# A stream of its own for the key projection's weights, woven into the merge of a transformer layer

## The chip, the cores and the metric

The kernel runs on one core of a Trainium2 chip. The metric is the device time of one execution in microseconds (us). Before the change three runs gave 2997.36 to 3000.63 us, with a median of 2999.9 us. For this kernel two times that differ by less than about 0.2% (6 us) can't be told apart.

The engines are named as in the profile: PE multiplies matrices, PEld loads its weights, DVE and ACT work on vectors, POOL is the general engine, SP issues most loads. Each engine takes its instructions strictly in the order of its queue, and an instruction that waits holds up everything behind it.

## The reference

The layer takes 1024 tokens and 256 context tokens, both of width 1024:

```python
h = rmsnorm(x, n1) * (1 + sc1) + sh1
q, k, v, gb, gcv, u, ga, gv = split_proj(h @ w_in)
y_attn = windowed_attention(rope(q), rope(k), v, kc, vc, sink) @ w_attn_out
y_conv = conv_branch(gb, gcv, u, conv_w, w_conv_out)
x = x + g1 * ((sigmoid(ga) * y_attn + sigmoid(gv) * y_conv) @ w_mix_out)
h2 = rmsnorm(x, n2) * (1 + sc2) + sh2
x = x + g2 * peer(h2, pw_q, p_keys, p_u, p_v)
return rmsnorm(x, final_g)
```

`peer` projects each token to 8 heads x 2 halves of 128 query values (`t @ w_q`, 1024 x 2048), scores each half against 128 keys (`sub_keys`), takes the best 16 of each half, the best 16 of their sums, and mixes 16 of 16384 experts per head by a softmax of the scores.

## The kernel before

**Precision by parts.** A float32 operand that PE multiplies is split into two float16 parts, high and low, and a product is three matmuls (`mm3`: high x high, high x low, low x high). For a weight this is done in `weight()`: SP loads a tile `w32` of 128 x 1024 float32 (512 KB), ACT casts it with a scale into the high part (below: the cast), DVE subtracts for the low part (the split), and both parts lie in a tile `whl`. With a key, POOL then issues a store of `whl` into a scratch tensor in HBM; the next call with that key loads the parts from there, by SP, without cast and split. There are two buffers for `w32` and four for `whl`, shared by all weights:

```python
w = self.pw.tile([128, 2, 8, 128], F16, name="whl", tag="whl", bufs=4)
w32 = self.pw.tile([128, 8, 128], F32, name="w32", tag="w32", bufs=2)
```

So a load into `w32` can't be issued before the split of the tile two loads earlier has read its buffer, and a cast can't start before a `whl` buffer is free: after its last matmul and its store.

**Stages.** The 1024 tokens are handled as two halves of 512. Stage 0 makes the modulation and the normed input. Stage 1 makes q, k, v and the convolution branch, woven with the attention of the first 4 of 8 blocks and with the late part of the modulation (the first weave). Stage 2 of half 0 has four pieces: the merge (8 steps of three weights each, `ga`, `gv`, `ac`), which is woven with the attention of blocks 4 to 7 (the second weave); the mixing projection (8 weights `mx`); the norm and modulation to `h2` (8 slices); and the key projection, 16 chunks `c`, each with one weight `wq`. A chunk is 24 matmuls of 128x512 on PE, a split of the product (`qqh` on ACT, `qql` on DVE), 12 short matmuls against a key table `sk` (one for chunks 0 to 7, one for 8 to 15), an eviction `sl` on ACT, and on DVE the search of the best 16 (`MAX`, `MAX_INDEX`, `MATCH_REPLACE`, 20 pieces). Stage 2 of half 1 follows with the same four pieces, beside it the selection and gate building of half 0 on DVE, PE and ACT (`run_side`, `gates`). It finds all weights in scratch. Then come the dense experts, two thirds of the time.

**Order.** `weave` advances several generators in turn, each by its share: with lengths 24 and 36 the merge gets 24 turns to the attention's 36. Within that order the framework's scheduler sets the final order of each engine's queue when the kernel is built. In `attends` the attention runs as a pipeline over 32 heads: scores of one head, transposes of the head before, sum of the head before that; between a head's scores and its transposes lie a maximum on DVE (`mx`, `nm`), an exponential on ACT (`pe`) and a split (`pn` on ACT and DVE).

**In the profile** most records carry line 72, the helper that forwards every call; so they are read by tiles: `whl<-w` on ACT is a cast, `whl<-w,whl` on DVE a split, `w<-w_q` on SP the load of a weight of the key projection.

Of the kernel before, what the change touches and what calls it, by code (L numbers as in the profile page):

```python
# [114 lines left out]
def drain(gen):  # L115
    while True:
        try:
            next(gen)
        except StopIteration as e:
            return e.value  # L120


class K:
# [678 lines left out]
    def natural(self, k):  # L802
# [8 lines left out]
        nc.scalar.activation(hn.rearrange("p a b -> p (a b)"), pt, AF.Copy)  # L811
        nc.sync.dma_start(self.h2d[:, :, k * 128:(k + 1) * 128].rearrange("t p d -> p t d"), hn)

    def scores(self, hf, c, qh, ql, skw):

        nc, p = self.nc, self.ps2
        ps = self.bank()
        for t in range(4):
            ts = slice(t * 128, (t + 1) * 128)
            self.mm3(ps[:, ts], qh[:, ts], ql[:, ts], skw[0][:, c % 8, :], skw[1][:, c % 8, :], True, True)  # L820
        sl = self.px1.tile([128, 4, 128], F32, name="sl", tag="sl", bufs=2)
        nc.scalar.activation(sl.rearrange("p a b -> p (a b)"), ps, AF.Copy, scale=2.0 ** -10)
        h, pp = c // 2, c % 2
        vs = [self.sv[hf][:, t, pp, h, :] for t in range(4)]
        ix = [self.si[hf][:, t, pp, h, :] for t in range(4)]
        for t in range(4):
            nc.vector.max(vs[t][:, 0:8], sl[:, t, :])
        for t in range(4):
            nc.vector.max_index(ix[t][:, 0:8], vs[t][:, 0:8], sl[:, t, :])
        for t in range(4):  # L830
            nc.vector.match_replace(sl[:, t, :], vs[t][:, 0:8], sl[:, t, :], NEG)
        for t in range(4):
            nc.vector.max(vs[t][:, 8:16], sl[:, t, :])
        for t in range(4):
            nc.vector.max_index(ix[t][:, 8:16], vs[t][:, 8:16], sl[:, t, :])
# [572 lines left out]
    def run(self):  # L1408
        nc, a = self.nc, self.a
        self.setup()  # L1410
        self.nsq = 4
        self.g_two, self.two = self.pool("psA", space=PSUM)
        self.g_pa, self.pa = self.pool("ps0", space=PSUM)
        self.nbank = 6
        g_pw, self.pw = self.pool("wts", side="left")
        halves = [None, None]
        self.hT, self.cT, self.aT = [None, None], [None, None], [None, None]
        for hf in (1, 0):
            g, p = self.pool(f"half{hf}", side="left")
            halves[hf] = g  # L1420
            self.hT[hf] = tuple(p.tile([128, 8, HALF], F16, name=f"hT{hf}{i}") for i in range(2))
            self.cT[hf] = tuple(p.tile([128, 4, HALF], F16, name=f"cT{hf}{i}") for i in range(2))
            self.aT[hf] = tuple(p.tile([128, 4, HALF], F16, name=f"aT{hf}{i}") for i in range(2))
        self.stage0()
        g_q, self.pq = self.pool("qkv", side="left")
        self.stage1()
        g_s2, self.ps2 = self.pool("s2", side="right")
        self.sv[0] = self.ps2.tile([128, 4, 2, 8, 16], F32, name="sv0")
        self.si[0] = self.ps2.tile([128, 4, 2, 8, 16], U32, name="si0")
        self.nrstd = 1  # L1430
        self.nsq = 2
        st = self.stage2(0)
        self.weave([(self.until(st, "merged"), 24), (self.attends(4, 8), 36)])
        self.close(g_q)
        self.close(self.g_pa)
        self.close(self.g_two)
        self.g_pa, self.pa = self.pool("psQ", space=PSUM)
        self.nbank = 8
        drain(self.until(st, "summed"))
        st1 = self.stage2(1)  # L1440
        for _ in range(8):
            next(st)
        for _ in range(AHEAD):
            next(st1)
        drain(st)
        self.close(self.g_pa)
        g_pf, self.pf = self.pool("psF", space=PSUM)
        self.ftag = ("f", 2)
        self.nbank = 6
        g_pa, self.pa = self.pool("psB", space=PSUM)  # L1450
        self.close(halves[0])
        g_g = self.open_gate("gate0", "left", 2)
        self.run_side(st1, self.gates(0), GATES_B)
        self.u_first = {i: self.weight(None, a["u_t"][i]) for i in range(UPRE, UPRE + 3)}
        self.close(g_g)
        self.close(self.g_x1)
        self.close(g_s2)
        self.close(halves[1])
        self.close(g_pw)
        self.close(g_pa)  # L1460
        self.close(g_pf)
        g_pv, pv = self.pool("psV", space=PSUM, reuse_waits="tile")
        self.pf, self.ftag = pv, ("v", 3)
        self.bank = self.fbank
        g_pt, self.ppt = self.pool("parts", side="left", reuse_waits="tile")
        g_ac, self.pac = self.pool("acc", side="left", reuse_waits="tile")
        self.part = self.pac.tile([128, 8 - NRES, HALF], F32, name="part")
        gd, pd = self.pool("dense0", side="left", reuse_waits="tile")
        g_g = self.open_gate("gate1", "right", 1)
        self.experts(pd, pv)  # L1470
        self.close(gd)
        self.close(g_ac)
        self.close(g_pt)
        self.close(g_g)
        self.close(g_pv)
        self.close(self.g_pc)
# [63 lines left out]
```

## Time and profile before

| what | value |
|---|---|
| median of 3 runs | 2999.9 us |
| the profiled execution's own time | 2997.38 us |
| its span, first to last instruction | 2995.6 us |
| busy: PE, DVE, ACT, POOL | 95%, 88%, 39%, 35% |
| second weave with its end | 339 to 517 us |
| mixing projection of half 0 | 517 to 561 us |
| norm and modulation of half 0 | 561 to 580 us |
| key projection of half 0 | from 567, searches done at 680.6 us |
| stage 2 of half 1 with the gates | to about 1060 us |

The times in the rows below count from the span's start. The share of busy time over the whole span says little, since the stages have different limits; it is read by stage. A bracket at the end of a row gives the idle time just before the instruction and what ended it.

### The profile page before, as it was taken

Reading aid. Unit: us, or ns where it says so; the run is one execution under the profiler, and the core shown is the slowest. Engines: PE = TensorE matmul, PEld = TensorE weight load, DVE = VectorE, ACT = ScalarE, POOL = GpSimd, SP = SyncE. Lnnn points to the kernel's source line nnn. Section 1 sums busy time; section 2 is a strip of 40 time slices with the busy share of each in tenths; the row PEclk is TensorE's granted clock in tenths of the full one; section 3 lists DMA queues with packets and bytes.
Section 4 is the critical chain, followed back from the end, with each engine's and each line's share of the span. In section 5 each row is a group of like instructions: output and inputs, shape, how many; then the busy total and the mean of one; then the engine's idle time right before and its main releaser. Section 6 shows DMA issues by size and latency. Waiting matters only on the chain.

```text
span 2995.6 us, 49091 instructions
## 1 busy us (share of the span) xinstructions
PE 2858.1 (95%) x18685; PEld 1521.8 (51%) x18685; DVE 2647.2 (88%) x5438; ACT 1176.0 (39%) x1878; POOL 1052.4 (35%) x814
## 2 busy tenths in 40 slices
PE   6899999989989998999999999999999999999998
PEld 2455555444444543444444444444444446776675
DVE  7788776699999999999899999999889979888887
ACT  4844576333434332332333333333333333433432
POOL 3200012201111004444444444544544444455553
PEclk9999999999999998999999999999999999999999
DMA  6233445654445728998999998999989999999995
GB/s 227 92 120 114 127 127 183 215 181 151 176 179 185 255 82 288 315 329 309 331 314 349 352 327 306 338 332 332 351 314 347 324 316 339 360 377 351 354 365 192
DMA packets 327197, 795.74 MB, mean 266 GB/s; under 512 B 22960, under 2 KB 147248, under 8 KB 319792
## 3 DMA queue, kind: packets, MB, share of 16 engines
q1 hardware_dynamic: 219536, 372.08, 37.4%
q0 software_dynamic: 103968, 395.36, 35.7%
q10 hardware_dynamic: 3456, 25.17, 2.1%
q8 instruction: 146, 2.39, 0.3%
q14 instruction: 91, 0.75, 0.1%
HBM read 696.31 MB, written 96.21 MB: 265 GB/s over the span
## 4 chain that ended last, share of the span: by engine, by line
PE 44%; DVE 10%; DMA 4%; issue 3%; POOL 2%; ACT 0%; SPq 0%; DVEq 0%; POOLq 0%; ACTq 0%
PE res L72 23%; PE ups L72 13%; PE vps L72 5%; DVE row L72 4%; DMA row<-u,ci 2%; POOL row L916 2%; PE fbank L72 1%; DVE vl L72 1%; DMA v<-v 1%; DVE ul L72 1%; DVE eq L72 1%; DVE wdl L72 1%; DVE gel L72 0%; DVE part L72 0%; ACT ge L72 0%
## 5 line engine op out<-in xcount | busy, mean ns | idle before, releaser
L916 POOL DMA_INDIRECT row<-u,ci x512 | 669.9, 1308 | 881.1 <-DVE row L72 649.4
L72 DVE SCALAR_TENSOR_TENSOR row<-row,hn 128x1024 f32<-128x1024 f32 x512 | 614.1, 1222 | 62.7 <-DMA row<-u,ci 46.0
L72 PEld LDWEIGHTS <-vh 128*128 128x128 f16 x5120 | 468.4, 98 | 341.4 <-issue 12.5
L72 PE MATMUL res<-wdl,vh 128*128 128x128 f16 (+2 forms) x2176 | 626.2, 305 | 14.3 <-DVE wdl L72 14.1
L72 PE MATMUL res<-wdh,vl 128*128 128x128 f16 (+2 forms) x2176 | 623.1, 305 | 6.7 <-DVE vl L72 6.7
L72 PE MATMUL res<-wdh,vh 128*128 128x128 f16 (+2 forms) x2176 | 622.8, 305 | 0.0
L72 PE MATMUL ups<-h,uh 128*128 128x512 f16 x1952 | 582.4, 380 | 0.0
L72 PEld LDWEIGHTS <-whl 128*128 128x128 f16 x3288 | 317.0, 99 | 368.7 <-issue 47.2
L72 PE MATMUL bank<-hT,whl 128*128 128x512 f16 x1584 | 376.2, 386 | 16.0 <-ACT hT L72 5.7
L72 ACT ACTIVATE vh<-v 128x1024 f16<-128x1024 f32 x248 | 260.3, 1050 | 296.1 <-PE res L72 143.1
L72 PE MATMUL ups<-h,ul 128*128 128x512 f16 x976 | 371.0, 380 | 5.1 <-DVE ul L72 5.1
L72 PEld LDWEIGHTS <-vl 128*128 128x128 f16 x2560 | 250.5, 98 | 197.2 <-DVE vl L72 27.7
L72 PEld LDWEIGHTS <-uh 128*128 128x128 f16 x1952 | 190.9, 98 | 228.5 <-issue 2.7
L72 DVE SCALAR_TENSOR_TENSOR vl<-v,vh 128x1024 f16<-128x1024 f32 x248 | 301.7, 1217 | 0.1
L916 POOL DMA_INDIRECT row<-v,ci x128 | 210.9, 1648 | 179.6 <-DVE wdl L72 90.0
L72 ACT ACTIVATE gel<-ups 128x512 f32<-128x512 f32 x125 | 74.6, 597 | 370.8 <-PE ups L72 341.7
L72 ACT ACTIVATE ge<-fbank 128x512 f32<-128x512 f32 x224 | 122.2, 594 | 245.7 <-PE fbank L72 228.4
L72 ACT ACTIVATE wdh<-gel 128x512 f16<-128x512 f32 x128 | 80.5, 629 | 342.5 <-DVE gel L72 328.1
L72 DVE SCALAR_TENSOR_TENSOR racc<-row,fig,racc 128x1024 f32<-128x1024 f32 x127 | 162.5, 1280 | 10.7 <-DMA row<-v,ci 9.7
L72 DVE TENSOR_TENSOR e<-iotas,ii 128x1024 f16<-128x1024 f16 x224 | 153.0, 705 | 6.9 <-ACT ii L72 4.8
L72 PEld LDWEIGHTS <-ul 128*128 128x128 f16 x976 | 95.7, 98 | 121.9 <-DVE ul L72 6.5
L72 PE MATMUL vps<-wdh,vh 128*128 128x512 f16 x384 | 145.5, 379 | 4.3 <-ACT ge L72 3.6
(223 smaller groups left out, 4191.1 us busy)
## 6 DMA issues: line engine op xcount, KB each, us to landing
v<-v SPq DMA_DIRECT2D x248, 512.0 KB
u<-u_t SPq DMA_DIRECT2D x122, 512.0 KB
gd<-ge POOLq DMA_DIRECT2D x32, 1024.0 KB
gt<-gd SPq DMA_DIRECT2D x32, 1024.0 KB
wm<-w_mod SPq DMA_DIRECT2D x48, 512.0 KB
gd<-ge ACTq DMA_DIRECT2D x24, 1024.0 KB
gt<-gd SPq DMA_DIRECT2D x32, 768.0 KB
w<-w_in SPq DMA_DIRECT2D x34, 512.0 KB
```

The costliest lines, as they stand in the source:

```text
L72: r = f(*args, **kw)
L916: self.nc.gpsimd.indirect_dma_start(out=r, out_offset=None, in_=tab, in_offset=bass.IndirectOffsetOnAxis(ap=ci[:, s:s + 1], axis=0))
```

## The change

A generator `key_weights` calls `weight()` for the two key tables and the 16 weights of the key projection, one per turn, and is woven into the second weave as a third stream with 18 turns. Its result is not kept: what stays is the copy in scratch. When the key projection of half 0 calls `weight()` with the same keys, it finds them there.

```diff
+    def key_weights(self):
+
+        for c in range(18):
+            if c < 2:
+                self.weight(("sk", c), self.a["skT"][c], scale=64.0)
+            else:
+                self.weight(("wq", c - 2), self.a["w_q"][c - 2])
+            yield
@@
-        self.weave([(self.until(st, "merged"), 24), (self.attends(4, 8), 36)])
+        self.weave([(self.until(st, "merged"), 24), (self.attends(4, 8), 36), (self.key_weights(), 18)])
```

So 18 loads, casts, splits and stores move from the key projection (and the end of the mixing projection, where the first were loaded) into the second weave and the end of the first. In the key projection 18 loads of parts from scratch take their place.

The ACT queue in the middle of the second weave, before. `w_5044` and `w_5127` are weights of the merge, `pe` and `pn` belong to the attention, `sgv` and `sa` are gates.

```order
L72 ACTIVATE whl<-w_4920 128x1024
L72 ACT_TABLE_LOAD
L72 ACTIVATE sgv<-bank 128x512
L72 ACTIVATE ao<-sc 128x64
L72 ACT_TABLE_LOAD
L72 ACTIVATE pe,se<-sc,nm 128x640
L72 ACTIVATE whl<-w_5044 128x1024
L72 ACTIVATE pn<-pe 128x640
L72 ACTIVATE whl<-w_5127 128x1024
L72 ACTIVATE mh<-sa 128x512
```

The same place now. `w_4904`, `w_4990` and `w_5121` are weights of the merge, `w_4983` and `w_5114` weights of the key projection.

```order
L72 ACTIVATE whl<-w_4904 128x1024
L72 ACTIVATE whl<-w_4983 128x1024
L72 ACT_TABLE_LOAD
L72 ACTIVATE sgv<-bank 128x512
L72 ACTIVATE ao<-sc 128x64
L72 ACT_TABLE_LOAD
L72 ACTIVATE pe,se<-sc,nm 128x640
L72 ACTIVATE whl<-w_4990 128x1024
L72 ACTIVATE pn<-pe 128x640
L72 ACTIVATE whl<-w_5114 128x1024
L72 ACTIVATE ao<-sc 128x64
L72 ACTIVATE whl<-w_5121 128x1024
```

Five casts stand where three stood, and the attention's `pe` and `pn` stand between and behind them.

The DVE queue in one chunk of the key projection of half 0, before: a split of a weight follows each `qql`.

```order
L72 SCALAR_TENSOR_TENSOR qql<-bank,qqh 128x512
L72 SCALAR_TENSOR_TENSOR whl<-w_6702,whl 128x1024
L72 MAX sv_3545<-sl 128x8 x4
L72 MAX_INDEX si_3546<-sv_3545,sl 128x8 x4
L72 MATCH_REPLACE sl<-sv_3545,sl 128x128 x4
L72 MAX sv_3545<-sl 128x8 x4
L72 MAX_INDEX si_3546<-sv_3545,sl 128x8 x4
```

The same chunk now.

```order
L72 SCALAR_TENSOR_TENSOR qql<-bank,qqh 128x512
L72 MAX sv_3545<-sl 128x8 x4
L72 MAX_INDEX si_3546<-sv_3545,sl 128x8 x4
L72 MATCH_REPLACE sl<-sv_3545,sl 128x128 x4
L72 MAX sv_3545<-sl 128x8 x4
L72 MAX_INDEX si_3546<-sv_3545,sl 128x8 x4
```

The split is gone from every chunk; the rest stands as it stood. PE's queue has the same instructions in nearly the same order.

## Rows read from the trace of the kernel before

**Rows 1.** Busy time by stage: busy us (instructions) per engine, clock, DMA share, GB/s

```profile
180.00:339.00 159.00, 155.80 (x1438) 93.20 (x1437) 137.13 (x240) 67.83 (x136) 2.38 (x4) 1.00 0.40 120
339.00:517.00 178.00, 171.93 (x1571) 99.39 (x1569) 125.65 (x196) 127.02 (x209) 30.13 (x37) 1.00 0.46 142
...
580.00:681.00 101.00, 93.11 (x553) 46.89 (x553) 100.19 (x543) 30.67 (x46) 7.46 (x14) 0.97 0.60 194
681.00:1060.00 379.00, 345.61 (x2425) 182.08 (x2424) 361.99 (x1145) 152.37 (x249) 57.95 (x54) 0.98 0.53 187
```

**Rows 2.** Groups in 580 to 681: busy us, mean ns, then idle before and releaser

```profile
L72 DVE SCALAR_TENSOR_TENSOR whl<-w,whl 128x1024 f16<-128x1024 f32 x14 | 17.1, 1219 | 0.8 <-ACT whl L72 0.8
...
L72 ACT ACTIVATE whl<-w 128x1024 f16<-128x1024 f32 x14 | 14.8, 1054 | 23.9 <-DMA w<-w_q 23.9
...
L72 PE MATMUL bank<-whl,qql 128*128 128x128 f16 x64 | 12.1, 226 | 7.1 <-DVE qql L72 7.1
```

**Rows 3.** Timeline of PE, one chunk of the key projection: start, duration, instruction

```profile
642.23 5.34 PE L72 MATMUL bank<-h,whl 128*128 128x512 f16 x24
...
647.41 0.27 PE L72 MATMUL bank<-whl,qqh 128*128 128x128 f16 x2
...
648.06 0.23 PE L72 MATMUL bank<-whl,qql 128*128 128x128 f16 x1 [0.38 <-DVE qql L72]
...
648.63 5.34 PE L72 MATMUL bank<-h,whl 128*128 128x512 f16 x24
```

**Rows 4.** Timeline at the first and the last chunks of the key projection

```profile
575.45 1.22 DVE L72 SCALAR_TENSOR_TENSOR whl<-w,whl 128x1024 f16<-128x1024 f32 x1
...
577.38 2.33 PE L72 MATMUL bank<-h,whl 128*128 128x512 f16 x10 [0.25 <-DVE h L72]
...
661.43 5.34 PE L72 MATMUL bank<-h,whl 128*128 128x512 f16 x24
...
671.39 0.29 PE L72 MATMUL bank<-whl,qql 128*128 128x128 f16 x1 [3.65 <-DVE qql L72]
...
673.38 7.18 PE L72 MATMUL bank<-hT,whl 128*128 128x512 f16 x24 [0.73 <-ACT sl L72]
...
680.61 0.27 DVE L72 CAST fi<-si 128x256 f16<-128x256 uint32 x1
```

**Rows 5.** Timeline of SP and ACT: two loads of a weight and the casts they release

```profile
622.42 0.33 SPq L172 DMA_DIRECT2D w<-w_q  x1
...
627.69 1.06 ACT L72 ACTIVATE whl<-w 128x1024 f16<-128x1024 f32 x1 [4.78 <-DMA w<-w_q]
...
641.06 0.33 SPq L172 DMA_DIRECT2D w<-w_q  x1
...
645.14 1.06 ACT L72 ACTIVATE whl<-w 128x1024 f16<-128x1024 f32 x1 [3.34 <-DMA w<-w_q]
```

**Rows 6.** Groups of DVE and ACT in the second weave, 339 to 517

```profile
L72 DVE SCALAR_TENSOR_TENSOR whl<-w,whl 128x1024 f16<-128x1024 f32 x23 | 31.3, 1360 | 5.2 <-ACT whl L72 5.1
...
L72 ACT ACTIVATE whl<-w 128x1024 f16<-128x1024 f32 x24 | 25.2, 1051 | 14.7 <-PE bank L72 14.7
L72 ACT ACTIVATE pe<-sc,nm 128x640 f32<-128x640 f32 x23 | 18.2, 794 | 5.0 <-DVE nm L72 4.8
L72 ACT ACTIVATE pn<-pe 128x640 f16<-128x640 f32 x23 | 16.2, 728 | 0.2
L72 ACT ACTIVATE ao<-sc 128x64 f32<-128x64 f32 x32 | 6.9, 217 | 5.3 <-PE sc L72 5.0
```

**Rows 7.** Timeline in the second weave: a cast that waits, and PE behind it

```profile
423.78 1.06 ACT L72 ACTIVATE whl<-w 128x1024 f16<-128x1024 f32 x1 [1.75 <-PE bank L72]
...
425.18 1.72 DVE L72 SCALAR_TENSOR_TENSOR whl<-w,whl 128x1024 f16<-128x1024 f32 x1
...
426.65 0.30 PE L72 MATMUL sc<-kd,q 128*128 128x320 f16 x1 [1.24 <-ACT ao L72]
...
429.25 0.61 PE L72 MATMUL sc<-v,pt 128*128 128x64 f16 x15 [1.78 <-DVE pt L72]
```

## The prediction

> **What bounds the kernel now.** I read the busy times by stage first, then the groups of the two stages that the change touches, then the timelines there. In the second weave PE is busy 171.9 of 178 us, and ACT and DVE 127 and 126: PE sets the pace, with 6.1 us of idle time [rows 1]. In the key projection of half 0 it is the other way round: DVE is busy 100.2 of 101 us, PE 93.1 [rows 1]. The 14 splits in that stretch are 17.1 us of this, and ACT waits 23.9 us for the loads of weights, which costs nothing there, since DVE is late anyway [rows 2]. Half 1 behind it has DVE busy 362 of 379 us and PE 346 [rows 1]: DVE is nearer to full, so what DVE gets back at 680.6 us, where it turns from the searches to the selection [rows 4], should mostly reach the end. The dense stage needs the result of all this and simply starts earlier or later.
>
> **What the change takes out of the key projection.** One chunk takes 648.63 - 642.23 = 6.40 us [rows 3]. PE's own work in it is 5.18 us of projection (642.23 to 647.41) and 12 short matmuls: ten of them take 648.63 - 648.06 = 0.57 us, so 12 about 0.68 [rows 3]; together 5.86. DVE's is 6.40 with the split and 6.40 - 1.22 = about 5.2 without [rows 2, 3]. So PE takes over as the bound at 5.86, and not all of the 18 x 1.22 = 22 us that DVE sheds comes back.
>
> The sum for the stage: the first two chunks run while the modulation still makes `h2`, and their last matmuls end at 577.38 + 2.33 = 579.7 [rows 4]. A split of 1.22 us stands among the modulations at 575.45 [rows 4] and goes: 578.5. Fourteen chunks follow: 14 x 5.86 = 82.0, so PE ends the last projection at 660.5, where it now ends at 661.43 + 5.18 = 666.6 [rows 4]. In the old order PE then waits 3.65 us for `qql` behind the searches and takes 7.18 us for the next 24 matmuls [rows 4], where 5.18 is usual: a stretch at 1.2 instead of 2.4 GHz. With DVE in step the last `qql` follows at once; the two searches left on DVE, of 4.6 us each (the 5.2 without a `qql` of 0.6), end at about 660.5 + 1.2 + 9.2 = 671. That is 10 us before 680.6; PE turns to half 1 some 11 us earlier. I take a gain of 10 us. Bounds: 4, if only the 6.3 us on PE come through and half 1 swallows a third; 22, if all of DVE's relief did. The 18 loads from scratch that stand in place of the old ones are cost at nothing: in half 1 the same loads feed the same chunks, and PE's waits in this kernel's key projections are for DVE and not for a load. If one came late, it would cost up to a load time, 4 to 5 us.
>
> **What it puts into the second weave.** Each moved weight brings a load, a cast, a split and a store; 17 more casts fall between 339 and 517 us (24 now, 41 then; by the queue, the other moves end in the first weave). Busy time: ACT 127 + 17 x 1.05 = 145 us, DVE 126 + 17 x 1.36 = 149 [rows 1, 6], both under 178. Traffic: 142 GB/s x 178 us is 25 MB, and 18 weights of 1.05 MB (load and store) make it 44 MB, or 248 GB/s; by the key projection's 194 GB/s at a share of 0.60 that is a share of about 0.77 [rows 1]. None of this alone is over the limit.
>
> What is near a limit is the loop through the two `w32` buffers. A load was issued at 622.42 and its cast, which waited for it, began at 627.69: 5.3 us; another took 645.14 - 641.06 = 4.1 [rows 5]. Behind the landing come the cast (1.05) and the split: from the cast at 423.78 to the split's end at 426.90 there are 3.1 us [rows 7]; at least it is 1.05 + 1.2 = 2.3. So one buffer comes round in 6.4 to 8.4 us, and a weight passes every 3.2 to 4.2 us, where the weave asks for one every 178 / 41 = 4.3. On the average it holds, but the queue isn't even. Take the piece of the new ACT queue that the change section shows: between the start of the cast of `w_4990` and that of `w_5121` ACT has two casts, a `pn` and an `ao`, 1.05 + 0.73 + 1.05 + 0.22 = 3.05 us [rows 6]; but the load of `w_5121` goes out only behind the split of `w_4990`, 6.4 to 8.4 us before its own cast can start. ACT stands for 3 to 5 us, and behind it wait `mh`, `pe` and `pn`: the softmax of the next heads, on which PE's transposes wait. I went down the queue this way, with 4.5 us for a load and 3.0 for cast and split: 16 of the 41 casts come too soon, by 40 us in all. With 4.1 and 2.4 it is 13 casts and 26 us, with 5.3 and 3.7 it is 19 and 60 us. In the old queue the same count gives 5 us.
>
> How much of it PE feels: casts already wait 14.7 us for buffers [rows 6], and PE idles 6.1 us in all. The rows show the way: a cast waits 1.75 us, and 1.8 us after it ends PE idles 1.24 us for `ao`, then 1.78 us for `pt` [rows 7]. 6.1 / 14.7 = 0.41 us of PE for 1 us of a waiting cast. 40 x 0.41 = 16 us; since ACT's slack shrinks from 51 to 33 us, I take 17. Bounds: 0, if the cover of PE's long projections holds, and 40, if all of it passes through.
>
> The sum: 2997.4 (the profiled execution; its span of 2995.6 and 1.8 around it) - 10 + 17 = 3004.4. The median of the runs is 2.5 above that execution, so 3007 is what I compare with 2999.9.
>
> [...]
>
> **The rivals.**
>
> (1) The weave hides everything: 2997.4 - 10 = 2987, 2990 as a median. For it: in the first weave DVE is busy 137 of 159 us, 86%, and PE still 155.8 (98%) [rows 1], beside steady loads on the same SP queue. Against it: ACT has 68 of 159 us there, and in the new second weave 145 of 178; few of those loads go through cast and split. It decides if PE loses under 4 us in the weave.
>
> (2) A draw: loads near 4.1 us and a prompt DVE, 26 x 0.41 = 11 us lost, 10 gained: 2998, 3001 as a median. For it: the 4.1 us load; against it: the larger share of DMA in the weave.
>
> (3) Heavily slower: ACT falls so far behind that every stall reaches PE, and `whl` buffers, of which four now serve two streams, come late for the merge itself; 40 us lost, 10 gained: 3027, 3030 as a median. It begins where ACT's waits pass its slack of 33 us. For it: PE's clock fell behind a wait of 3.65 us [rows 4], so stalls of that length would cost twice. Against it: PE has 5.18 us of projection between most steps of the attention as cover.
>
> That the change does not do what it says is excluded by the order: no cast and no split is left in the key projection.
>
> **How the numbers follow.** I give the forecast 42%, rival (1) 25%, the draw 22%, (3) 11%. What counts as no change is within 0.2%, 2994 to 3006. The forecast's own range is 3002 to 3015, as its weave loss goes from 12 to 25; about 8 of its 42 points lie under 3006. So slower is 34 + 11 = 45%, the same 22 + 8 = 30%, faster 25%. The range for 8 in 10 reaches down to rival (1), 2989, and up to (3), 3030.
>
> **What would show it.** In the profile after: chunks of the key projection 5.9 us apart and PE busy without a break there, with DVE idle in between; the `CAST` of the selection some 10 us closer to the first chunk. In the second weave: casts that wait for `w<-w_q` and `w<-w_in`, which they don't at all now, in sum some 30 to 40 us; PE idle 20 us and more, before transposes and sums, released by ACT and DVE; the stage from 339 to 534 instead of 517. I am wrong if casts hardly wait for loads, or wait and PE's idle time stays near 6 us: then (1) holds. I am wrong about the gain if chunks stay at 6.4 us, or if half 1 takes up what they save.

## The result and the profile after

The changed kernel takes 3018.55 us (median of 4 runs, 3017.22 to 3019.65), the kernel before, beside it on the same chip, 2998.63 us (4 runs, 2995.23 to 3000.63). The ratio is 1.0067 with a 95% interval of 1.0055 to 1.0079: slower by 20 us, where 7 were predicted (3007, with a range of the forecast itself from 3002 to 3015 and one for 8 in 10 from 2989 to 3030). The profiled execution of the changed kernel took 3017.84 us, with a span of 3016.1.

Where the 20.5 us of the two spans lie (the stages are bounded by first instructions: `sa` of the merge, `mh` into the mixing projection, `qqh` of the key projection, the selection's `CAST`, the first `wdl<-gel` of the dense stage and its last one):

| stage of half 0 | before | after | difference |
|---|---|---|---|
| up to the merge (first weave) | 339.2 | 343.2 | +4.0 |
| second weave | 178.3 | 199.6 | +21.3 |
| mixing projection, norm | 61.2 | 60.1 | -1.1 |
| key projection | 101.9 | 96.1 | -5.8 |
| half 1 with the gates | 409.3 | 406.6 | -2.7 |
| dense stage | 1359.7 | 1365.3 | +5.6 |
| what follows | 546.0 | 545.2 | -0.8 |

The busy times by stage, after; as in [rows 1] the columns are PE, PEld, DVE, ACT and POOL busy, granted clock, DMA share, GB/s:

```profile
343.20:542.80 199.60, 176.56 (x1568) 101.14 (x1567) 142.37 (x209) 137.71 (x220) 38.37 (x54) 0.97 0.65 209
605.00:699.00 94.00, 91.23 (x558) 46.69 (x556) 86.56 (x528) 18.74 (x32) 0.00 (x0) 1.00 0.35 125
```

In the second weave PE is idle for 199.6 - 176.6 = 23.0 us; before it was 178.3 - 171.8 = 6.5, counted the same way. That is 16.5 us of the 21.3. The other 4.8 are in the busy time: the same matmuls take 176.6 instead of 171.8 us, and the granted clock beside them is 0.97 instead of 1.00: it falls to 0.50 (1.2 of 2.4 GHz) in three places, around 400, 445 and 482 us, each beside a wait of PE (2.5, 3.9 and 3.9 us). In the key projection the roles have changed as against [rows 1]: PE is busy 91.2 of 94 us, DVE has idle time.

One chunk of the key projection on PE, after, for [rows 3]:

```profile
641.95 5.34 PE L72 MATMUL bank<-h,whl 128*128 128x512 f16 x24
...
647.80 5.34 PE L72 MATMUL bank<-h,whl 128*128 128x512 f16 x24
```

The chunk takes 647.80 - 641.95 = 5.85 us, without a wait; before it took 6.40. The weights now come from scratch, and two groups in 605 to 699 show what PE waits for:

```profile
L72 PE MATMUL bank<-h,whl 128*128 128x512 f16 x336 | 74.8, 379 | 1.6 <-DMA whl<-ws_wq 1.6
...
L72 PE MATMUL bank<-whl,qql 128*128 128x128 f16 x62 | 11.2, 219 | 0.4 <-DVE qql L72 0.4
```

The 7.1 us of waiting for `qql` [rows 2] are 0.4, and PE waits 1.6 us in all for the loads of parts.

Casts and splits in the second weave, after, for [rows 6]:

```profile
L72 DVE SCALAR_TENSOR_TENSOR whl<-w,whl 128x1024 f16<-128x1024 f32 x39 | 50.5, 1300 | 22.2 <-ACT whl L72 21.9
L72 ACT ACTIVATE whl<-w 128x1024 f16<-128x1024 f32 x40 | 41.5, 1053 | 34.3 <-DMA ws_wq<-whl 22.2 <-PE bank L72 4.5 <-DMA w<-w_ac 4.1
```

And all waits of the casts in 343.2 to 542.8 (us in total, times, longest), with the longest ones of PE:

```profile
ACT whl L72 <- DMA ws_wq<-whl: 22.2, 10, 4.1
PE sc L72 <- ACT ao L72: 6.9, 4, 3.9
PE sc L72 <- ACT pn L72: 5.2, 5, 2.8
PE sc L72 <- DVE pt L72: 4.7, 2, 3.9
ACT whl L72 <- PE bank L72: 4.5, 2, 3.9
ACT whl L72 <- DMA w<-w_ac: 4.1, 2, 2.4
ACT whl L72 <- DMA w<-w_mx: 1.5, 1, 1.5
ACT whl L72 <- DMA w<-w_in: 1.3, 1, 1.3
ACT whl L72 <- DMA w<-w_q: 0.6, 1, 0.6
```

The casts wait for a DMA, but hardly for a load: 7.5 us in four rows. What they wait for is `ws_wq<-whl`, the stores of the new stream, 22.2 us; about half of it, 11 us in five waits, stands in front of casts of the merge, the rest in front of the stream's own (loads and casts paired in their order). For PE, which held their buffers before, they wait 4.5 us instead of the 14.7 of [rows 6]; in all 34.3 instead of 14.7. A store holds its parts buffer `whl` until it has landed, and the next cast wants that buffer. The DMA issues in 343 to 543 (count, KB each, median us from issue to landing) give the time:

```profile
ws_wq<-whl POOLq DMA_DIRECT2D x16, 512.0 KB, 5.4
```

The timeline at the end of the weave shows such a wait and who stands behind it:

```profile
528.16 0.56 POOL L176 DMA_DIRECT2D ws_wq<-whl  x1 [2.54 <-DVE whl L72]
...
533.43 1.06 ACT L72 ACTIVATE whl<-w 128x1024 f16<-128x1024 f32 x1 [4.13 <-DMA ws_wq<-whl]
534.40 0.61 ACT L72 ACTIVATE oh<-ao 128x512 f16<-128x512 f32 x1
...
535.07 0.40 PE L72 MATMUL bank<-id,oh 128*128 128x128 f16 x4 [1.70 <-ACT oh L72]
...
536.41 0.40 PE L72 MATMUL bank<-id,ol 128*128 128x128 f16 x4 [0.94 <-DVE ol L72]
```

The store goes out at 528.16 and the cast begins at 533.43. Behind the cast in ACT's queue stands `oh` of the attention, and PE idles 1.70 us for it, then 0.94 for `ol`, which DVE makes from it.

### The profile page after: what moved, and what is told of

Its sections match the earlier page's. It is cut to its first block, busy times and chain, and to the rows that moved or that the text cites. A ratio compares the mean times of both kernels' runs of the same rounds, so it can differ in the third digit from the quotient of the medians.

```text
span 3016.1 us, 49116 instructions
## 1 busy us (share of the span) xinstructions
PE 2862.5 (95%) x18685; PEld 1524.1 (51%) x18685; DVE 2650.1 (88%) x5438; ACT 1171.0 (39%) x1876; POOL 1057.6 (35%) x814
## 4 chain that ended last, share of the span: by engine, by line
PE 41%; DVE 9%; issue 5%; DMA 4%; POOL 3%; ACT 0%; POOLq 0%; DVEq 0%; ACTq 0%
PE res L72 23%; PE ups L72 12%; PE vps L72 5%; DMA row<-u,ci 3%; DVE row L72 3%; POOL row L925 3%; PE fbank L72 1%; DVE vl L72 1%; DVE ul L72 1%; DVE wdl L72 1%; DVE eq L72 1%; DVE gel L72 0%; ACT ge L72 0%; DVE part L72 0%; DVE acc L72 0%
## 5 line engine op out<-in xcount | busy, mean ns | idle before, releaser
L72 PEld LDWEIGHTS <-vh 128*128 128x128 f16 x5120 | 469.0, 98 | 342.6 <-issue 15.0
L72 ACT ACTIVATE gel<-ups 128x512 f32<-128x512 f32 x125 | 74.6, 597 | 351.0 <-PE ups L72 339.9
## 6 DMA issues: line engine op xcount, KB each, us to landing
gt<-gd SPq DMA_DIRECT2D x32, 1024.0 KB, 12.2
gt<-gd SPq DMA_DIRECT2D x32, 768.0 KB, 10.3
```

What stands on the lines that cost most here:

```text
L72: r = f(*args, **kw)
```

## The experiments

Each was run beside the kernel before; the ratio is to that, with its 95% interval. Theories in the expectations: A, the stores hold the shared parts buffers; B, the loop through the two `w32` buffers (my prediction); C, the plain work of the added casts and splits; D and E are told where they come in. The framework orders the queues anew for each kernel: costonly has the ACT queue of the changed kernel from 300 us to the end of the second weave, operation by operation (250), but in nostore, noload, workonly and ownwhl1 19 to 34 of these stand elsewhere, and on DVE 30 to 51 of some 260 (compared in the traces). What these four give for a part of the stream holds the effect of the other order too, and no run takes the two apart.

**costonly: the stream without its use.** The stores go under other names, so the key projection loads and splits everything as before.

```
-                self.weight(("sk", c), self.a["skT"][c], scale=64.0)
+                self.weight(("zk", c), self.a["skT"][c], scale=64.0)
-                self.weight(("wq", c - 2), self.a["w_q"][c - 2])
+                self.weight(("zq", c - 2), self.a["w_q"][c - 2])
```

> The woven stream does all its 18 loads, casts, splits and stores, but stores under other names, so that the key projection of half 0 loads, casts and splits as in the kernel before. This is the cost alone. If cost and gain are separate and add up, the second weave is as long as in the changed kernel (mixing projection starting near 542 us, PE idle there some 22 us), chunks of the key projection are 6.4 us apart, and the total lies 20 + 10 = 30 us over before. Rival: what the weave loses is partly given back later in any case, and the total is only 20 us over before.

Measured: 3030.41 us, ratio 1.0098 (1.0074 to 1.0122). The second weave, with the columns as above:

```profile
343.80:548.00 204.20, 180.99 (x1565) 103.17 (x1563) 142.15 (x208) 137.79 (x219) 38.63 (x53) 0.94 0.66 210
```

The two parts of the change add up: +31 us for the cost alone, +20 for both, so a gain of about 11 (9.6 by the stages of the two profiles before and after). PE's idle time is that of the changed kernel (23.2 against 23.0 us), while its busy time is 4.4 us longer at a clock of 0.94: with the same order of ACT's queue, the idle time came out alike in the two profiles and the clock did not.

**nostore: the stream without its stores** (their key is `None`); the key projection as before.

```
-                self.weight(("wq", c - 2), self.a["w_q"][c - 2])
+                self.weight(None, self.a["w_q"][c - 2])
```

> The woven stream loads, casts and splits the 18 weights but does not store the parts, and the key projection makes its own again as before. Theory A (a shared buffer of parts is held by the store of a key weight, and a cast of the next weight stands until that store has landed): without stores the casts hardly wait for a buffer, the second weave gets back 15 of the 21 us it lost, the total is some 10 us over before. Theory B (the loop through the two float32 buffers, as I predicted): the weave stays some 20 us longer and the total is near that of the cost alone, 30 over before, with casts waiting for loads. Theory C (just more work on ACT and DVE): as B, but no waits for loads.

Measured: 3011.75 us, ratio 1.0038 (1.0022 to 1.0054). The second weave, and the waits of casts in it:

```profile
340.30:527.80 187.50, 174.81 (x1571) 100.29 (x1570) 140.82 (x211) 140.53 (x224) 31.27 (x38) 0.99 0.55 174
```

```profile
ACT whl L72 <- DMA w<-w_mx: 8.1, 4, 3.8
...
ACT whl L72 <- DMA w<-w_in: 1.8, 2, 0.9
ACT whl L72 <- DMA w<-w_q: 1.7, 2, 0.9
```

Against costonly the weave gets 16.7 us back and the first weave 3.5. With all loads in place and no store it loses only 9.2 us, where theory B expected some 20. The casts wait 12.2 us for loads, with the 0.6 for `w_ac` that is not shown; PE idles 12.7 us, 6.2 more than before.

**noload: the stream without its loads.** One float32 tile of its own is loaded once; 18 casts, splits and stores under other names follow from it. The key projection is as before.

```
+        w32 = self.pk.tile([128, 8, 128], F32, name="w32k", tag="w32k", bufs=1)
+        self.nc.sync.dma_start(w32, self.a["skT"][0])
...
+            self.split(w32, 64.0, w[:, 0], w[:, 1])
```

> The woven stream loads one float32 tile once into a buffer of its own and casts, splits and stores it 18 times, under other names; the key projection makes its own parts as before. So the 17 other loads, and their use of the two shared float32 buffers, are left out. Theory A (stores hold the buffers of parts): the weave is as long as with the loads, total 25 to 30 us over before. Theory B (loads): the weave is back to within 5 us of before, total some 5 us over before. Theory C (work on ACT and DVE): 25 to 30 over before, without waits of casts for stores.

Measured: 3015.05 us, ratio 1.0048 (1.0026 to 1.0069).

```profile
339.30:536.00 196.70, 179.14 (x1548) 102.40 (x1548) 150.13 (x214) 145.69 (x228) 41.60 (x58) 0.95 0.57 188
```

```profile
ACT whl L72 <- DMA ws_z<-whl: 11.2, 6, 2.8
```

The loads are gone and the weave still loses 18.4 us. Two things make this number too large: the profiled execution, 3021.0 us, is the slowest of the five (from 3007.78), and 4.3 us of it are a wait of PE that the edit itself brings (workonly, next). What is left for the loads is told with the table below.

**workonly: neither loads nor stores.** The edit is noload without its store. Theory D had come from the runs so far (ACT's idle time in front of a DMA is what reaches PE, at about a half), and it expected next to nothing here.

> The stream with its 18 casts and splits alone: they read one resident float32 tile, nothing is loaded per weight and nothing is stored; the parts buffers are the shared four, the key projection is as before. Theory D (PE idles some 0.5 us for each us that a cast on ACT stands for a DMA; the bare work costs nothing): casts wait for DMA under 5 us, PE idles 6 to 9 us in the second weave, which takes 178 to 182 us; total 0 to +5 against before (3001 to 3006). Theory C (the work of the added casts and splits on ACT and DVE costs by itself): weave 186 to 190 us as without the stores, total +9 to +12 (3011).

Measured: 3010.96 us, ratio 1.0033 (1.0020 to 1.0046).

```profile
340.40:530.00 189.60, 177.13 (x1548) 101.05 (x1548) 144.69 (x214) 144.61 (x228) 33.17 (x40) 0.96 0.49 148
```

```profile
ACT whl L72 <- PE bank L72: 10.7, 6, 4.5
...
PE bank L72 <- ACT whl L72: 4.3, 1, 4.3
```

The weave loses 11.3 us, as theory C expected, and 6.0 of it are idle time of PE. But the wait of 4.3 us is not plain work. It belongs to this edit and to noload alone, and stands at the head of the stream:

```profile
337.99 1.06 ACT L72 ACTIVATE whl<-w32k 128x1024 f16<-128x1024 f32 x1 [4.51 <-DMA w32k<-skT]
...
343.05 1.04 ACT L72 ACTIVATE whl<-w 128x1024 f16<-128x1024 f32 x1
...
344.15 1.03 PE L72 MATMUL bank<-hT,whl 128*128 128x512 f16 x2 [4.29 <-ACT whl L72]
```

The first cast of the stream waits for the load of the one resident tile, a cast of the merge stands behind it in ACT's queue, and PE waits for that one; the granted clock is 0.50 in 343 to 349 us. Without this wait some 4 to 7 us would be left for plain work, an estimate (11.3 less 4.3, and less up to 3 for those 6 us at half the clock). So this run doesn't decide between C and D. D's half fits most of the other kernels: casts wait 29.7 us for DMAs in the changed kernel and PE idles 16.5 more than before, in costonly 29.3 and 16.7, in ownwhl1 27.9 and 14.8, in nostore 12.2 and 6.2, in half 15.2 and 4.6. It doesn't fit streampool (52.9 and 43.4), and no run changes these waits alone.

The four kernels give the parts of the loss, with the reservation on the order. Each field has the length of the second weave (178.3 without a stream), and in brackets how much later than before the mixing projection starts, so with the first weave, and how much longer the median of the whole kernel is:

| | no store | with store |
|---|---|---|
| no load | 189.6 (12.5; 10.9) | 196.7 (18.5; 15.6) |
| with load | 187.5 (10.3; 12.3) | 204.2 (30.5; 31.0) |

The field with both is costonly; the changed kernel, whose median holds the gain too, has 199.6 (25.3). Neither stores nor loads alone come near the whole: stores without loads add 5 to 7 us to the work, loads without stores next to nothing. Beside each other they do: the stores add 15 to 20 us where the loads are there (12 to 17 in the second weave), the loads 7 to 15 where the stores are (3 to 8 there), and rather more for the wait in the row without loads. So the loads have a part in the loss, though casts hardly wait for them; with them casts wait 20.9 us for stores, without them 11.2. How they do it was not tried.

**ownwhl1: one parts buffer more, for the stream alone.** Two or more were not tried.

```
+        w = (self.pk.tile([128, 2, 8, 128], F16, name="whl", tag="whl", bufs=1) if own
+             else self.pw.tile([128, 2, 8, 128], F16, name="whl", tag="whl", bufs=4))
```

> The changed kernel, with one parts buffer more that only the key stream uses; the merge keeps its four. Theory A (the stores of the key stream hold the shared parts buffers, and so the casts of the merge stand): the merge's casts no longer wait for key stores; the key stream's own casts wait for its single buffer, about 1.1 (cast) + 1.4 (split) + 0.6 (issue) + 5.4 (store) = 8.5 us per weight against a turn of 11 us, so now and then. Second weave 187 to 192 us (before 178, changed 200), total 3005 to 3011. Theory B (loads and their two buffers): nothing changes, weave 198 to 201, total 3016 to 3020. Theory C (plain work of the added instructions): as B.

Measured: 3014.81 us, ratio 1.0053 (1.0032 to 1.0074).

```profile
338.30:539.60 201.30, 180.00 (x1588) 103.24 (x1585) 146.42 (x215) 144.75 (x227) 42.21 (x58) 0.97 0.71 226
```

```profile
ACT whl L72 <- DMA ws_wq<-whl: 15.6, 8, 4.2
ACT whl L72 <- DMA w<-w_in: 6.9, 6, 2.6
```

Theory A missed the weave: I expected 187 to 192 us and it is 201.3. The waits for stores fall by 7 us only; all of them now stand in front of the stream's own casts, which share one buffer, and the waits for `w_in` rise by 6. The first weave takes 338.3 us, but it is another first weave: the first key table's store goes out at 338.11 us there, in the changed kernel at 314.33, so this says nothing of the sharing. In the second weave the merge's casts are free of the stores and little is won; ACT stands as well when a cast of the stream has to wait. Whether two buffers of its own would help, this run doesn't tell.

**streampool: the stream's split by POOL alone.** Cast and split leave ACT and DVE.

```
+            if pool:
+                nc.gpsimd.tensor_scalar(w32, w32, float(scale), None, op0=ALU.mult)
+                nc.gpsimd.tensor_copy(w[:, 0], w32)
+                nc.gpsimd.tensor_tensor(w[:, 1], w32, w[:, 0], op=ALU.subtract)
```

> The changed kernel, but the stream's cast and split are done by POOL alone (scale in place, copy to float16, subtract; some 2.2 us each, 18 x 6.5 = 117 us of POOL, which had 30 of 178 us). ACT and DVE see nothing of the stream; loads, stores and the shared buffers stay. Theory D (the loss comes about because ACT stands in its queue for a DMA, and PE idles about 0.5 us for each us of it): the casts of the merge wait for DMA under 10 us, PE idles 6 to 11 us in the second weave, which takes 178 to 186 us; total 2989 to 2999, faster than both kernels. Rival E (the shared buffers or the traffic are what costs, whichever engine splits): the buffers are held longer, since POOL is slower and the merge's stores queue behind it; casts wait 30 us and more, weave 200 us or longer, total 3015 to 3030.

Measured: 3053.9 us, ratio 1.0181 (1.0163 to 1.0200), the slowest of all.

```profile
343.40:580.90 237.50, 187.56 (x1588) 107.49 (x1584) 138.95 (x196) 126.79 (x208) 135.90 (x101) 0.91 0.56 174
```

```profile
ACT whl L72 <- DMA ws_wq<-whl: 39.6, 9, 6.8
...
ACT mh L72 <- POOL sa L744: 17.2, 5, 9.2
```

Rival E came true, and beyond its range of 3015 to 3030. None of the stream's work is on ACT, and yet ACT waits 39.6 us for its stores: these are the merge's casts, which want the shared buffers that the stream now holds longer. Two of the merge's own jobs, its additions (`sa`) and its stores, queue on POOL behind the stream.

**half: 9 of the 18 weights in the stream.**

```
-        for c in range(18):
+        for c in (0, 2, 3, 4, 5, 6, 7, 8, 9):
```

> The changed kernel with 9 of the 18 weights in the stream (key table 0 and weights 0 to 7 in 9 turns); the other 9 are split in the key projection as before. Theory A (buffers overrun by stores): waits for stores fall by more than half, under 12 us of the 31.5; the weave loses 6 to 9 us, the key projection gains about 5, total +1 to +6 (3000 to 3006). Theory C (each moved weight costs the same): 12.6 lost, 5 gained, total +8 (3008).

Measured: 3003.0 us, ratio 1.0011 (0.9999 to 1.0022), within theory A's range. The weave loses 6.3 us and the first weave 2.0; at the start of the dense stage 4.2 of these 8.3 are back. Half of the stream costs a third of it. But the two weights of the next run cost the second weave as much as these nine, so the loss doesn't simply follow their number.

**gainonly: the use without most of the stream.** Only one table and one weight are made in the stream, and all chunks take that pair; the other 15 weights and the second table are left out.

> The woven stream makes only the first key table and the first of the 16 key weights, and all chunks of the key projection in both halves load that one pair of parts from scratch: 14 other weights and the second table are left out of the computation. So the key projection has the traffic and queues of the changed kernel, and the weave nearly those of before. If the gain is what I worked out (DVE free of the splits, PE the bound at 5.86 us a chunk, half 1 passing it on) the total is 8 to 12 us below before. Rival: half 1 swallows it, and the total is within 4 us of before.

Measured: 3006.5 us, ratio 1.0021 (1.0005 to 1.0037): a miss, I expected less than before. The ten runs fall into two groups, four from 2998.33 to 2999.76 us and six from 3006.05 to 3012.13, and the profile is of the first group (2999.35), so its stages don't show the 7 us. In it the weave takes 184.5 us (+6.2, for two weights), from the mixing projection to the dense stage the kernel gains 13.5 us (key projection 96.3, half 1 402.5), and then the dense stage takes 1370.6 us, 10.9 more than before, in which nothing was changed.

Yet this run shows the path from a store to PE more plainly than the others. From 300 us to the end of the second weave 233 of ACT's 234 operations stand in the order of the kernel before. One store of the stream is followed by this, as lines of POOL, ACT and PE and the row of the stretch behind:

```profile
404.95 0.57 POOL L176 DMA_DIRECT2D ws_sk<-whl  x1 [1.39 <-DVE nm L72]
...
409.93 1.06 ACT L72 ACTIVATE whl<-w 128x1024 f16<-128x1024 f32 x1 [3.47 <-DMA ws_sk<-whl]
...
413.06 0.30 PE L72 MATMUL sc<-kd,q 128*128 128x320 f16 x1 [3.38 <-ACT ao L72]
```

```profile
414.20:417.20 3.00, 3.00 (x19) 1.38 (x17) 1.97 (x4) 2.99 (x6) 0.53 (x1) 0.50 0.94 332
```

A cast of the merge waits 3.47 us for the store, `ao` of the attention stands behind it, PE idles 3.38 us for `ao`, and then runs at a granted clock of 0.50. In the kernel before PE has no wait above 0.2 us in 400 to 416.

**before_again: the kernel before, profiled once more.**

> The kernel before, once more, for a second profile of it. If the dense stage's length differs from one profile to the next of the same kernel, it comes out some 5 us off 1359.7; if the 5.6 us that the changed kernel lost there belong to its order, it is 1359 to 1361 again. Second weave 178 us either way.

Measured: 3001.42 us. The second weave takes 178.2 us and the key projection 101.6, as they did, the dense stage 1362.0 against 1359.7 and half 1 411.7 against 409.3. So 2 us of such a stage vary without a change; the first weave of poolsplit, which nothing was changed in, took 342.6 us against 339.2 and 339.9.

**poolsplit and poolsplit2: the same gain by another way.** No stream; in the key projection of half 0 POOL makes the low parts. In poolsplit ACT scales the tile and casts it, in poolsplit2 ACT casts and POOL scales.

```
+            if pool:
+                nc.scalar.activation(w[:, 0], w32, AF.Copy, scale=float(scale))
+                nc.gpsimd.tensor_scalar(w32, w32, float(scale), None, op0=ALU.mult)
+                nc.gpsimd.tensor_tensor(w[:, 1], w32, w[:, 0], op=ALU.subtract)
```

> The kernel before, without a stream; only in the key projection of half 0 the split is taken from DVE another way: ACT scales the loaded tile and casts it, and POOL subtracts. If the gain of the change is DVE's relief and nothing else, the key projection shortens as in the changed kernel, by 5 to 6 us with 10 at the start of the dense stage, and nothing is lost in the weave: total -6 to -12 (2988 to 2994). Rival: POOL's subtraction is late for PE (a weight every 5.9 us; POOL some 2 to 4 us for it) or slows DVE beside it: key projection 100 to 105 us, total 0 to +5.

> As poolsplit (the kernel before, no stream, the low part of the key projection's weights made by POOL), but POOL does the scaling too, so that ACT has its one cast as before. If ACT's additional operation in front of the modulations and the evictions was what cost poolsplit its gain: norm stage 61 us again, key projection 96 to 98, total 2990 to 2996. Rival: POOL needs 2 x 2.2 + 0.6 = 5 us a weight and holds a loaded tile so long that the loads come late: key projection 102 to 108 us, total 3003 to 3012, as poolsplit.

Measured: 3008.96 us, ratio 1.0033 (1.0019 to 1.0047), and 3003.23, ratio 1.0008 (0.9997 to 1.0019). poolsplit misses both of its ranges; poolsplit2 lies at the lower edge of its rival's (3003 to 3012). The scaling on ACT and the row of PE at the first chunks of poolsplit, then POOL's group in 570 to 681 of poolsplit2 and one line from its norm:

```profile
573.36 1.06 ACT L72 ACTIVATE w<-w 128x1024 f32<-128x1024 f32 x1 [4.53 <-DMA w<-w_q]
...
576.98 7.07 PE L72 MATMUL bank<-h,whl 128*128 128x512 f16 x23 [5.61 <-ACT h L72]
```

```profile
L175 POOL TENSOR_SCALAR w<-w 128x1024 f32<-128x1024 f32 x15 | 41.7, 2782 | 9.5 <-ACT whl L72 9.2
```

```profile
560.04 1.26 POOL L330 TENSOR_TENSOR sq<-sq 128x512 f32<-128x512 f32 x1
```

In poolsplit the scaling, which waits for a load, stands in ACT's queue in front of the modulation `h`, and PE idles 5.61 us. In poolsplit2 POOL needs 2.8 us to scale and 2.2 to subtract, and squares of the norm (`sq`), which are POOL's work too, stand behind that in its queue: the last begins at 560.04 us where it began at 555.65 before, ACT's `rstd` behind it 3.9 us later, and the stage up to the key projection takes 66.6 us instead of 61.2. That loads come late, as the rival had it, shows less there: two casts wait 4 to 5 us for one. DVE was relieved in both (busy 78 and 84 of 101 us); it didn't help, since another wait took its place.

**altsplit: every second weight by POOL**, from the fourth on; the rest by DVE as before.

```
-            w = self.weight(("wq", c), a["w_q"][c])
+            w = self.weight(("wq", c), a["w_q"][c], pool=c >= 3 and c % 2 == 1)
```

> The kernel before without a stream; in the key projection of half 0 every second weight from the fourth on (7 of 16) has its low part made by POOL (2.8 + 2.2 us of each 11.7), the others and the tables by DVE as before. DVE has 5.2 + 0.6 = 5.8 us per chunk on the average, as much as PE's 5.86, and no tile is held longer than its turn. Expected: norm stage 61 us, key projection 96 to 99, total -3 to -8 (2993 to 2998), faster than both kernels. Rival: POOL's long hold of a loaded tile delays the next load as in poolsplit2: key projection 101 to 103, total 0 to +4.

Measured: 2995.88 us, ratio 0.9985 (0.9973 to 0.9997). It is the one version that beats both kernels, by 0.15%, which is less than the 0.2% that a single comparison tells apart, though the interval leaves out 1. POOL's first scaling begins here at 581.10 us, behind the norm. Its key projection:

```profile
580.00:681.00 101.00, 96.47 (x574) 48.88 (x573) 98.13 (x565) 33.24 (x48) 42.44 (x28) 0.97 0.62 202
```

```profile
628.46 5.34 PE L72 MATMUL bank<-h,whl 128*128 128x512 f16 x24
...
634.31 5.34 PE L72 MATMUL bank<-h,whl 128*128 128x512 f16 x24
```

PE is busy 96.5 us where it was 93.1 [rows 1], the chunk takes 5.85 us, and the stage 97.4 us instead of 101.9, with nothing put into the weave.

## Why the prediction was right and wrong

**The gain: right.** A chunk of 5.86 us was predicted, 5.85 measured; PE took over from DVE. 10 us were to reach the end of half 1, and 25.3 - 15.7 = 9.6 did (the lag at the start of the mixing projection, less that at the start of the dense stage). The way there differs a little: the selection came 7 us closer, not 10, and half 1 added 2.7 instead of swallowing some; its first 24 matmuls took 5.34 us instead of the 7.18 of [rows 4], where PE's wait of 3.65 us before them is now 0.44.

**Nothing for the loads from scratch: nearly right**, 1.6 us of PE in the stage.

**The weave's loss: right in sign, too small, and by the wrong buffers.** The step that failed is "what is near a limit is the loop through the two `w32` buffers". Casts were to wait 30 to 40 us for loads; they wait 7.5, and 22.2 for the stores of the stream. Without stores and with every load the weave loses 9.2 us; without loads it still loses some 11 to 14 (18.4 with the wait that noload brings, counted as in workonly). I had named the four `whl` buffers for two streams in the rival of a heavy loss only, and had priced no store in the forecast: its 5.4 us to landing appear nowhere in my count. The path behind a waiting cast, through ACT's queue to the attention and PE, was right, and gainonly shows it. The idle time of PE came out near the forecast (16.5 us more, 17 predicted, and "20 us and more" in all), but that is partly luck: 40 us of waits for loads at 0.41 were predicted, and 29.7 us for DMAs, three quarters of them stores, at 0.56 came. The 0.41 was taken from waits for buffers that PE held, a kind of wait that shrank to 4.5 us.

**Plain work at nothing: too low, the size open.** The prediction found ACT and DVE under their limits in the sum and cost the casts and splits themselves at nothing. nostore puts 9.2 us there for work and loads together, workonly 11.3, of which some 4 to 7 are left without its own load. That an operation which others wait for comes late when additional ones stand before it in its queue, though the engine has idle time in the sum, is the likely cause; it was not isolated.

**The clock: left out of the sum.** The prediction mentions that a stall can cost twice, in a rival, and counts none of it. PE's busy time in the weave grew by 4.8 us at a clock of 0.97; in the other kernels with a stream it grows by 2 to 9 us, and most where PE idles most (streampool: 15.8 at 0.91). With the idle time and the first weave this makes up the loss: 16.5 + 4.8 + 4.0 = 25.3 us, where 17 were predicted.

**The first weave at nothing: wrong by 4.0 us.** There casts wait 9.3 us for stores of the key tables, two waits, and PE idles 5.1 us for the attention's `pt`, 3.1 of it in one wait right behind the first of them. costonly, with the same stores, took 343.8 us, nostore 340.3. But a first weave varies by up to 3 us by itself (poolsplit).

**The dense stage: not foreseen, and open.** +5.6 us. DVE, ACT and POOL have the same instructions in the same order there in both kernels. Without a stream it took 1359.7 to 1363.7 us (five profiles, three of them with other splits), with one 1361.0 to 1370.6 (nine); the ranges overlap, and the cause wasn't found.

In sum, for the profiled execution: 3004.4 predicted, + 8.3 (17 became 25.3 in the two weaves, by the three terms above) + 0.4 (the gain) + 4.8 (the dense stage and what follows) = 3017.9; 3017.84 is measured. Slower was right, but the measured 3018.55 lies above the forecast's own range, which ends at 3015. Rival (1) is refuted by PE's 23.0 us of idle time and the draw by the interval. The rival of a heavy loss named the right buffers but not the size.

## What to carry to other kernels

Work that is moved into a stage with idle engines is not free: count for each moved operation what stands behind it in its queue, and price that with experiments that leave out its loads, its stores and both. Look at the first instructions of each such edit, since one load left at its head cost up to 4.3 us here, and compare the order of the queues. Where results are kept in memory, the store belongs in the loop of its buffer: a buffer is held until the store has landed, 5.4 us here, where a load took 4.3. If only one engine is over its share in a stage, moving every second piece to another engine in place can do more than moving all of it elsewhere (altsplit against poolsplit2; the gain on the kernel before is 0.15% only).

## What the runs showed of the hardware

**DVE and POOL.** POOL needs 2.8 us to scale 128x1024 float32 and 2.1 to subtract (streampool; 2.8 and 2.2 in poolsplit2); a split takes DVE 1.22 us [rows 2]. When POOL is busy with this, some operations of DVE get slower and others don't. Groups of DVE in the second weave, before:

```profile
L72 DVE COPY pt<-sc 128x1280 f16<-128x1280 f16 x24 | 19.5, 814 | 0.3 <-PE sc L72 0.2
L72 DVE TENSOR_REDUCE mx<-sc 128x1 f32<-128x640 f32 x23 | 18.9, 821 | 14.6 <-PE sc L72 14.3
L72 DVE SCALAR_TENSOR_TENSOR pn<-pe,pn 128x640 f16<-128x640 f32 x23 | 18.7, 831 | 14.4 <-ACT pn L72 14.4
```

The same groups in streampool, 343 to 580:

```profile
L72 DVE SCALAR_TENSOR_TENSOR pn<-pe,pn 128x640 f16<-128x640 f32 x23 | 26.3, 1163 | 15.6 <-ACT pn L72 15.6
L72 DVE COPY pt<-sc 128x1280 f16<-128x1280 f16 x24 | 19.6, 815 | 0.9 <-PE sc L72 0.7
L72 DVE TENSOR_REDUCE mx<-sc 128x1 f32<-128x640 f32 x23 | 18.8, 819 | 7.9 <-PE sc L72 7.8
```

`pn`, which reads two tiles from SBUF, goes from 831 to 1163 ns in the mean; the copy and the maximum, which read one from PSUM, stay as they were. The mean mixes two kinds: the 12 `pn` with no work of POOL beside them took 811 to 826 ns, the 11 beside some 816 to 3231. The split reads two tiles from SBUF as well: in the kernel before, it took 1.21 to 1.23 us alone and up to 1.97 beside POOL, which is how the mean of 1.36 in [rows 6] comes about. The Trainium skill ("SBUF — State Buffer", section "Who interferes with whom") says that an operation of DVE with two SBUF inputs contends with one of GpSimd that reads SBUF, and that one with at most one such input does not, outside DVE's two-port modes; the trace agrees (831 to 1163 ns against 814 to 815 and 821 to 819).

**Stores and loads.** A store of the stream (512 KB) landed 5.4 us after its issue in the changed kernel. In noload, where the stream's loads are missing, it is (345 to 520):

```profile
ws_z<-whl POOLq DMA_DIRECT2D x16, 512.0 KB, 3.6
```

Yet the merge's stores take 5.4 to 5.6 us in that same stretch; why the two differ was not tried.
